# Keeping the transposed input of a two-block transformer kernel in DRAM instead of transposing it twice

## The chip, the cores and the metric

The kernel runs on one core of one Trainium2 chip. A core has five engines that run side by side, each working through its own list of instructions in order: TensorE (PE) for matrix products and transposes, VectorE (DVE), ScalarE (ACT), GpSimd (POOL), and SyncE (SP), which here only starts transfers. They meet through semaphores. The metric is device time of one execution in microseconds (us).

## The reference

Two transformer blocks follow each other on 512 tokens of width 1024, in float32. The part that matters here is the start and end of the first block's token mixer, and the memory projection of the second block, which the kernel does first of all:

```
h    = rmsnorm(x, norm_mix)                 # x: 512 x 1024
x    = x + hybrid_token_mixer(h, w_in, ...) # an mLSTM half and an RWKV half, then @ w_out
h    = rmsnorm(x, norm_x)                   # cross attention, feed-forward, ...
kv_m = rmsnorm(mem_2, g_mem_2) @ w_mem_kv_2 # 256 x 1024, from the second block
```

`rmsnorm(x, g)` is `x * rsqrt(mean(x*x) + 1e-6) * g`, row by row.

## The kernel before

Activations stand transposed in the kernel: model width on the 128 partitions, in 8 tiles (`KD`) of 128, and the 512 tokens along the free dimension. A float32 product is made of three passes: both operands are split into a rounded high part and a low part (`whi`, `wlo` for weights, `hh`, `hl` for activations), and high x high, high x low and low x high are added up in PSUM. A weight unit of 128x512 is loaded by SP into `wraw` (5 buffers), rounded by ACT into `whi`, and the rest made by DVE into `wlo` (3 buffers each).

A tile framework orders the instructions of each engine from the program order and priorities, and gives each its waits. Where `self.pinned` names an engine (`"pa"` in the opening: PE and ACT), that engine keeps the program's order. Tiles of a pool that was closed give their memory to later pools; an instruction that writes such memory waits for the last users of what lay there.

**The opening** (`start`, line 366). `x` and `mem_2` are loaded with tokens on partitions (`tok`). DVE or ACT sums squares, DVE computes `rs = rsqrt(mean + eps)` for six blocks of 128 tokens and multiplies each block of `x` by its `rs` in place (`scale`). The memory projection runs in two panels of 512 columns (`ch`), each in 8 steps over `k` of six matmuls. The steps of the second panel alternate with `turn` (line 461), which transposes tile `k` of the scaled `x` by four PE transposes into one PSUM bank (`p` and `q`, two of each) and evicts it twice: ACT writes `hh` (scaled by the norm's gain), DVE writes `hl` = the product less `hh`. Two further blocks of tokens, `mem`, are turned into `memT` in the same pool `st` and stored to `mem_kept`, and `kv_kept` holds the second block's memory keys and values. Both are DRAM tiles.

**The RWKV preparation** (`rwkv_prep`, line 570). Dense blocks of 24 matmuls follow each other on PE, one for every 128 columns of `w_in`. `shift` evicts a block twice on ACT (`sh`, whose first column POOL sets to 0, and `own`) and mixes them on DVE. The first shifted block becomes `lx`, the right side of the low-rank matmuls (`rank`), whose weights `lw`, `lwl` POOL prepares at the start, with `rst32`, a row pattern for a scan.

**The mixer's end** (`mixer_early`, line 1250, and `mixer_out`, line 1278). `x` is loaded a second time, tokens on partitions. The output projection goes over 8 tiles `m` of the result; behind the matmuls of each, four transposes of `x` go to a PSUM bank, ACT evicts them (`xs`, tile name `k`), and DVE adds them to the product in `xT`. ACT and DVE then make `hh` and `hl` of the cross attention from it.

Of the kernel before, what the change touches and what calls it, by code (L numbers as in the profile page):

```python
# [8 lines left out]
F32 = mybir.dt.float32  # L9
# [3 lines left out]
OP = mybir.AluOpType  # L13
# [3 lines left out]
S = 512  # L17
D = 1024
NB = S // 128
KD = D // 128  # L20
# [12 lines left out]
OE = 4  # L33
MY = 2
# [42 lines left out]
def weave(*gens):  # L77
    for _ in woven(*gens):
        pass
# [20 lines left out]
class Build:  # L100
# [265 lines left out]
    def start(self, st, yT, kept, hh, hl):  # L366
# [60 lines left out]
        ws = weights()  # L427
        wus = [next(ws), next(ws)]
        for ch, dst in ((0, km), (1, vm)):
            pss = [self.pm() for _ in range(2)]  # L430
            for k in range(KD):
                wu = wus.pop(0)
                wus.extend(part(ws, 1))
                self.dense_tok(pss, wu, (mh, mlo), (k,), k == 0, k == KD - 1, 512)
                if ch == 0:
                    if k < 3:
                        for b in range(2):
                            square((xs + m2)[(2 * k + 4 + b) % 6], (2 * k + 4 + b) % 6, b)
                    elif k == 3:
                        norms(0, 6)  # L440
                    else:
                        scale(xs[k - 4], k - 4)
                else:
                    self.turn(xs, k, k + 1, hh, hl, gc[:, 8:16])
            for s2 in range(2):
                self.act(dst[:, s2], pss[s2], AF.Copy, scale=rs[:, 4 + s2:5 + s2])
        self.pinned = ""
        self.head_norm(st, km, 4, 128, gkm, 2)
# [11 lines left out]

    def turn(self, xs, k0, k1, hh, hl, g):

        n = 128 * len(xs)
        per = 512 // n
        for k in range(k0, k1, per):
# [8 lines left out]
            if hl is not None:  # L474
                for m, pv, gm in cols:
                    self.stt(hl[:, m], pv, gm, hh[:, m].bitcast(F32), OP.mult, OP.subtract)


    def mixer(self, yT, hpool, kept):
# [13 lines left out]
        with tc.tile_pool(name="rk", bufs=1, reuse_waits=RW) as rk:  # L493
# [30 lines left out]
            with tc.tile_pool(name="ml", bufs=1, reuse_waits=RW) as ml:  # L524
# [6 lines left out]
                with tc.tile_pool(name="mid", bufs=1, reuse_waits=RW) as mid:  # L531
# [7 lines left out]
                    with tc.tile_pool(name="chain", bufs=1, reuse_waits=RW) as ch:  # L539
                        self.pinned = PIN[1]  # L540

                        self.turns = ["p", "s", "p", "y"]
                        weave(steps(CS, self.rwkv_chain(ch, TT, yT)), steps(XS + MY - LS - PS + 4 * OE, lstm, self.mixer_early(yT, rk)))
                self.pinned = ""
                self.turns, self.mms = ["p"], ["mm", "mm", "q", "q"]
                self.mixer_out(yT, rk, ml)

# [701 lines left out]

    def mixer_early(self, xT, rk):  # L1250

        nc, i = self.nc, self.i
        while not self.rw.get("read"):
            yield None
        x = self.tile(rk, [128, NB, D], "BK", 1)
        y = [self.tile(rk, [128, 2, 4, S], "KR", 1, F32R), None]
# [11 lines left out]
        parts(0)  # L1268
        for b in range(NB):
            nc.sync.dma_start(x[:, b], i["x"][0, 128 * b:128 * b + 128, :])  # L1270
        self.mms = ["mm", "mm", "q", "q"]
# [5 lines left out]

    def mixer_out(self, xT, rk, ml):
        x, y, half, early = self.outs
        y[1] = self.tile(rk, [128, 2, 4, S], "Gm", 1, F32R)  # L1280
        self.parts(1)
        for m in range(KD):
# [6 lines left out]
            for _ in half(ps, m, 1):  # L1289
                pass  # L1290
            p = self.pt()
            for b in range(NB):
                self.tr(p[:, 128 * b:128 * b + 128], x[:, b, 128 * m:128 * m + 128])
            xs = self.tile(ml, [128, 512], "k2", 2)
            self.act(xs, p)
            self.add(xT[:, m], xs, ps)

# [878 lines left out]
def kernel_body(ctx, tc, ins, out):  # L2176
# [4 lines left out]
    kd = ctx.enter_context(tc.tile_pool(name="kd", bufs=1, space=bass.MemoryType.DRAM))  # L2181
    kept = {n: kd.tile([128, 2048], F32, name=n + "_kept") for n in ("kv2", "mem", "k", "v")}
    ctx.enter_context(b.psum(mm=2, p=2, q=2, s=1, y=1))
    with tc.tile_pool(name="hp", bufs=1, reuse_waits=RW) as hp:
# [32 lines left out]
```

## Time and profile before

| | us |
|---|---|
| median of 3 runs | 1542.51 |
| lowest and highest | 1539.69, 1544.95 |
| the profiled execution, its own time | 1537.13 |
| its span, first to last instruction | 1535.4 |
| PE busy in the span | 1506.9 |
| DVE busy | 1082.0 |
| ACT busy | 748.7 |
| POOL busy | 98.9 |

The durations below come from the one profiled execution, whose time is 5.4 us under the median. A row of the timeline gives the start and the length of an instruction in us, its engine, its line in the kernel, output and inputs, and in brackets how long the engine had idled before it and what ended that. On PE the lengths overlap, since matmuls are pipelined: the distance from start to start counts there.

### The profile page before, as it was taken

How to read it: one execution, taken by the hardware profiler on the slowest of the kernel's cores; microseconds unless marked ns; L12 is line 12 of the kernel's file. 1: busy time of each engine (PE TensorE's matmuls, PEld its weight loads, DVE VectorE, ACT ScalarE, POOL GpSimd, SP SyncE). 2: the span in 40 equal slices, each digit the busy share in tenths (PEclk: the TensorE clock that was granted, in tenths of full speed). 3: DMA queues.
4: the chain of work that ended last, by engine and by line, in shares of the span. 5: the costliest groups of instructions: out<-in, count | busy, mean ns of one | idle time of the engine just before them, and what ended most of it. 6: DMA issues, size and time to landing. Idle time of an engine off the chain costs nothing.

```text
span 1535.4 us, 23728 instructions
## 1 busy us (share of the span) xinstructions
PE 1506.9 (98%) x8487; PEld 1237.2 (81%) x8487; DVE 1082.0 (70%) x2536; ACT 748.7 (49%) x1469; POOL 98.9 (6%) x241
## 2 busy tenths in 40 slices
PE   7999999999999999999999999999999999999999
PEld 5777788798888888888888888898877877878877
DVE  7776698998856556524544578879999785766563
ACT  6645556566554444434432444456554454644431
POOL 7000402122000000000000001000000000000000
PEclk9999999999999999999999999999999999999999
DMA  7533222145533133333333334242322322324222
GB/s 254 145 73 81 52 63 56 45 122 158 153 111 100 51 96 97 96 96 97 97 100 98 93 107 103 62 122 71 91 71 68 83 69 67 80 75 124 69 83 96
DMA packets 209591, 144.85 MB, mean 94 GB/s; under 512 B 13492, under 2 KB 190787, under 8 KB 208960
## 3 DMA queue, kind: packets, MB, share of 16 engines
q1 hardware_dynamic: 208000, 141.66, 32.6%
q0 software_dynamic: 1280, 1.52, 0.5%
q8 instruction: 67, 1.10, 0.3%
q14 instruction: 52, 0.43, 0.1%
q10 hardware_dynamic: 192, 0.14, 0.0%
HBM read 134.90 MB, written 8.39 MB: 93 GB/s over the span
## 4 chain that ended last, share of the span: by engine, by line
PE 85%; DVE 9%; ACT 2%; issue 1%; DMA 1%; DVEq 0%; SPq 0%; ACTq 0%
PE mm L180 39%; PE q L180 28%; PE p L188 4%; PE p L191 3%; PE y L188 3%; PE s L180 2%; DVE wlo L158 2%; PE s L188 2%; PE q L188 2%; PE s L191 1%; PE q L191 1%; DVE lqk L158 1%; DVE madd L1832 1%; ACT whi L155 1%; DVE m L1831 1%
## 5 line engine op out<-in xcount | busy, mean ns | idle before, releaser
L155 ACT ACTIVATE whi<-wraw 128x512 fp32r<-128x512 f32 (+2 forms) x472 | 292.5, 622 | 534.5 <-PE mm L180 216.2
L158 DVE TENSOR_TENSOR wlo<-wraw,whi 128x512 fp32r<-128x512 f32 (+2 forms) x472 | 320.3, 680 | 186.1 <-ACT whi L155 181.4
L180 PE MATMUL mm<-hh,whi 128*128 128x512 f32 (+1 forms) x760 | 281.2, 386 | 1.8 <-DVE hh L158 1.1
L180 PE MATMUL mm<-hh,wlo 128*128 128x512 f32 (+1 forms) x696 | 265.3, 381 | 0.0
L180 PE MATMUL mm<-hl,whi 128*128 128x512 f32 x632 | 247.2, 391 | 0.0
L180 PEld LDWEIGHTS mm<-hh,whi 128*128 128x128 f32 x760 | 138.9, 189 | 29.2 <-issue 3.0
L180 PEld LDWEIGHTS mm<-hh,wlo 128*128 128x128 f32 x696 | 131.0, 188 | 25.4
L180 PEld LDWEIGHTS mm<-hl,whi 128*128 128x128 f32 x632 | 119.2, 189 | 22.4 <-issue 0.5
L180 PE MATMUL q<-hh,whi 128*128 128x512 f32 x272 | 106.2, 391 | 0.0
L180 PE MATMUL q<-hh,wlo 128*128 128x512 f32 x272 | 106.0, 390 | 0.0
L180 PE MATMUL q<-hl,whi 128*128 128x512 f32 x272 | 106.0, 390 | 0.0
L180 PE MATMUL q<-whi,hh 128*128 128x512 f32 (+2 forms) x176 | 66.8, 388 | 0.0
L180 PE MATMUL mm<-whi,hh 128*128 128x512 f32 (+2 forms) x168 | 65.5, 396 | 0.0
L180 PE MATMUL q<-wlo,hh 128*128 128x512 f32 (+2 forms) x160 | 60.9, 381 | 0.0
L180 PEld LDWEIGHTS q<-hh,wlo 128*128 128x128 f32 x272 | 51.1, 188 | 10.6
L180 PEld LDWEIGHTS q<-hl,whi 128*128 128x128 f32 x272 | 51.1, 188 | 10.5
L180 PEld LDWEIGHTS q<-hh,whi 128*128 128x128 f32 x272 | 51.1, 188 | 10.4
L180 PE MATMUL mm<-wlo,hh 128*128 128x512 f32 (+2 forms) x152 | 57.9, 381 | 0.0
L180 PE MATMUL q<-whi,hl 128*128 128x512 f32 (+2 forms) x144 | 54.7, 380 | 0.0
L180 PE MATMUL mm<-whi,hl 128*128 128x512 f32 (+2 forms) x136 | 51.6, 380 | 0.0
L155 ACT ACTIVATE at_sm<-at_sm,at_mx 128x128 f32<-128x128 f32 (+3 forms) x64 | 35.7, 559 | 21.3 <-DVE at_mx L1598 20.9
L176 DVE SCALAR_TENSOR_TENSOR fy<-fc,vcols,fy 128x512 f32<-128x512 f32 x44 | 33.0, 751 | 9.2 <-ACT fy L155 8.5
(761 smaller groups left out, 3123.3 us busy)
## 6 DMA issues: line engine op xcount, KB each, us to landing
wraw<-in_w_in_dram SPq DMA_DIRECT2D x172, 256.0 KB, 2.9
wraw<-in_f_up_dram SPq DMA_DIRECT2D x88, 256.0 KB, 2.9
wraw<-in_f_down_dram SPq DMA_DIRECT2D x40, 256.0 KB, 2.8
wraw<-in_x_wkv_dram SPq DMA_DIRECT2D x32, 256.0 KB, 3.1
wraw<-in_w_out_dram SPq DMA_DIRECT2D x32, 256.0 KB, 2.7
wraw<-in_w_branch_dram SPq DMA_DIRECT2D x24, 256.0 KB, 2.7
wraw<-in_w_mem_kv_dram SPq DMA_DIRECT2D x16, 256.0 KB, 4.3
wraw<-in_x_wq_dram SPq DMA_DIRECT2D x16, 256.0 KB, 2.8
```

Source lines behind the costliest of these rows:

```text
L155: self.pin("a", self.nc.scalar.activation(out, in_, func, **kw))
L158: self.pin("v", self.nc.vector.tensor_tensor(out, a, b, op=op))
L176: self.pin("v", self.nc.vector.scalar_tensor_tensor(out, a, s, b, op0=op0, op1=op1))
L180: ins = self.nc.tensor.matmul(out, lhsT=a, rhs=b, start=start, stop=stop)
L188: self.pin("p", self.nc.tensor.matmul(out, lhsT=a, rhs=b, start=start, stop=stop))
L191: self.pin("p", self.nc.tensor.transpose(out, in_, self.ident if ident is None else ident))
L1831: nc.vector.max(m8, acc)
L1832: nc.vector.match_replace(acc, m8, acc, -3e38)
```

## The change

In the opening, `turn` gets a function `keep` that is called for each tile behind its two evictions: ACT evicts the bank a third time, unscaled, into `xk` (four buffers); POOL multiplies it by `full`; and POOL starts its store into a new DRAM tile `x_kept`. Since the transposed tile carries `rs`, `full` has to undo that: `root` is (mean + eps) times `rs`, which is 1/`rs`, and `row` makes of it, by four transposes and an eviction, a tile with the 512 values along the free dimension on all partitions. `mixer_early` loads `x_kept` in four transfers in place of `x`, and `mixer_out` adds it as it is.

```diff
+        root = st.tile([128, NB], F32, name="root")
+        full = st.tile([128, S], F32, name="full")
+        def keep(k, p):
+            t = self.tile(st, [128, S], "xk", 4)
+            self.act(t, p)
+            nc.gpsimd.tensor_tensor(t, t, full, op=OP.mult)
+            nc.gpsimd.dma_start(kept["x"][:, S * k:S * k + S], t)
...
                     elif k == 3:
                         norms(0, 6)
+                        self.mul(root, ss[:, 0:NB], rs[:, 0:NB])
...
-                    self.turn(xs, k, k + 1, hh, hl, gc[:, 8:16])
+                    self.turn(xs, k, k + 1, hh, hl, gc[:, 8:16], keep)
             for s2 in range(2):
                 self.act(dst[:, s2], pss[s2], AF.Copy, scale=rs[:, 4 + s2:5 + s2])
+            if ch == 0:
+                self.row(full, root)
...
+            if keep is not None:
+                for m, pv, gm in cols:
+                    keep(m, pv)
...
-        x = self.tile(rk, [128, NB, D], "BK", 1)
+        x = self.tile(rk, [128, KD, S], "BK", 1)
...
-        for b in range(NB):
-            nc.sync.dma_start(x[:, b], i["x"][0, 128 * b:128 * b + 128, :])
+        for k in range(0, KD, 2):
+            nc.sync.dma_start(x[:, k:k + 2].rearrange("p k t -> p (k t)"), kept["x"][:, S * k:S * k + 2 * S])
...
-            p = self.pt()
-            for b in range(NB):
-                self.tr(p[:, 128 * b:128 * b + 128], x[:, b, 128 * m:128 * m + 128])
-            xs = self.tile(ml, [128, 512], "k2", 2)
-            self.act(xs, p)
-            self.add(xT[:, m], xs, ps)
+            self.add(xT[:, m], x[:, m], ps)
...
+    kept["x"] = kd.tile([128, KD * S], F32, name="x_kept")
```

Three places in the engines' order show what moves. ACT in the second panel, before (`whi` is a weight's high part, `hh` the scaled input's; `p` and `q` are PSUM banks):

```order
L155 ACTIVATE hh_83<-q_360,gcols 128x512
L155 ACTIVATE whi_369<-wraw_367 128x512
L155 ACTIVATE hh_83<-p_379,gcols 128x512
L155 ACTIVATE whi_388<-wraw_386 128x512
L155 ACTIVATE hh_83<-q_398,gcols 128x512
L155 ACTIVATE whi_407<-wraw_405 128x512
```

and in the changed program:

```order
L155 ACTIVATE hh_84<-p_374,gcols 128x512
L155 ACTIVATE xk_381<-p_374 128x512
L155 ACTIVATE whi_387<-wraw_385 128x512
L155 ACTIVATE hh_84<-q_397,gcols 128x512
L155 ACTIVATE xk_404<-q_397 128x512
L155 ACTIVATE whi_410<-wraw_408 128x512
L155 ACTIVATE hh_84<-p_420,gcols 128x512
```

Between `hh` of a tile and the next weight stands the third eviction of the same bank; its waits name DVE's `hl` of that tile.

POOL at the end of the opening, before (`TT` holds the low-rank weights as loaded):

```order
L520 DMA xt<-in_r_g_up_dram 32x512
L581 MEMSET rst_641 128x512
L591 CAST lw_645<-TT 64x512
L582 MEMSET rst_641 128x16
L592 CAST lw_645<-TT 64x512
L593 TENSOR_TENSOR lwl<-TT,lw_645 64x512
```

and in the changed program, where eight such pairs (the last two shown) stand between the loads and the preparation:

```order
L436 TENSOR_TENSOR xk_490<-xk_490,full 128x512
L437 DMA x_kept<-xk_490 128x512
L436 TENSOR_TENSOR xk_507<-xk_507,full 128x512
L437 DMA x_kept<-xk_507 128x512
L597 MEMSET rst_683 128x512
L607 CAST lw_687<-TT 64x512
L598 MEMSET rst_683 128x16
L608 CAST lw_687<-TT 64x512
L609 TENSOR_TENSOR lwl<-TT,lw_687 64x512
```

The preparation of the low-rank weights went behind the stores. PE at the start of `mixer_out`, before (`Gm` holds the second half of the mixer's output, `BK` the input):

```order
L180 MATMUL mm_4924<-KR_4908,wlo_5018 128x512
L180 MATMUL mm_4921<-Gm_5037,whi_5048 128x512
L191 MATMUL p_5064<-ident,BK_4907 128x128 x4
L180 MATMUL mm_4921<-Gm_5037,whi_5048 128x512
L180 MATMUL mm_4921<-Gm_5037,wlo_5047 128x512
```

and in the changed program:

```order
L180 MATMUL mm_4966<-KR_4950,wlo_5060 128x512
L180 MATMUL mm_4963<-Gm_5079,whi_5090 128x512 x2
L180 MATMUL mm_4963<-Gm_5079,wlo_5089 128x512
L180 MATMUL mm_4963<-Gm_5079,whi_5090 128x512 x2
L180 MATMUL mm_4963<-Gm_5079,wlo_5089 128x512
```

All eight groups of four transposes are gone; the matmuls keep their order.

## Rows read from the trace of the kernel before

**Rows 1.** Page, part 1: busy time, share of the span, instructions.

```profile
PE 1506.9 (98%) x8487; PEld 1237.2 (81%) x8487; DVE 1082.0 (70%) x2536; ACT 748.7 (49%) x1469; POOL 98.9 (6%) x241
```

**Rows 2.** Stretches: length, busy us (instructions) by engine, granted clock, DMA share, GB/s.

```profile
34.00:44.00 10.00, 10.00 (x58) 8.30 (x56) 9.79 (x27) 6.69 (x12) 1.22 (x6) 1.00 0.59 137
410.00:447.50 37.50, 37.50 (x179) 30.29 (x177) 20.26 (x30) 18.61 (x31) 0.00 (x0) 1.00 0.30 88
```

**Rows 3.** The same view: the slice with the lowest clock in the opening.

```profile
30.00:32.00 2.00, 2.00 (x6) 1.61 (x6) 1.89 (x4) 1.21 (x2) 1.88 (x3) 0.50 0.34 120
```

**Rows 4.** Timeline of PE, second panel: turns 0, 1 and 7.

```profile
29.78 0.47 PE L191 MATMUL p<-ident,tok 128*128 128x128 f32 x1 [1.29 <-DVE tok L171]
...
32.60 0.60 PE L191 MATMUL q<-ident,tok 128*128 128x128 f32 x4
...
43.60 0.60 PE L191 MATMUL q<-ident,tok 128*128 128x128 f32 x4
```

**Rows 5.** Timeline of PE in the output projection, around one group of transposes.

```profile
429.01 0.60 PE L191 MATMUL p<-ident,BK 128*128 128x128 f32 x4
...
430.14 0.63 PE L180 MATMUL q<-KR,whi 128*128 128x512 f32 x2
...
430.85 0.63 PE L180 MATMUL q<-KR,whi 128*128 128x512 f32 x2
```

**Rows 6.** Timeline of SP: the last of the four loads of `x`.

```profile
382.96 1.30 SPq L1270 DMA_DIRECT2D BK<-in_x_dram  x1
```

**Rows 7.** Tile `k` in 410 to 450 us: ns min/median/max, first and last start.

```profile
L155 ACT ACTIVATE k<-p x8: 574/598/601, 412.2 to 447.8; 128x512 f32<-128x512 f32 x8
```

**Rows 8.** Timeline of ACT in the second panel.

```profile
36.91 0.69 ACT L155 ACTIVATE hh<-q,gcols 128x512 fp32r<-128x512 f32 x1 [0.62 <-PE q L191]
37.49 0.62 ACT L155 ACTIVATE whi<-wraw 128x512 fp32r<-128x512 f32 x1
```

**Rows 9.** Timeline of DVE in the opening.

```profile
25.68 2.43 DVE L171 TENSOR_SCALAR tok<-tok,nt_rs 128x1024 f32<-128x1024 f32 x3
...
31.02 0.75 DVE L176 SCALAR_TENSOR_TENSOR hl<-p,gcols,hh 128x512 fp32r<-128x512 f32 x1
...
38.44 0.68 DVE L158 TENSOR_TENSOR wlo<-wraw,whi 128x512 fp32r<-128x512 f32 x1
...
49.88 1.42 DVE L171 TENSOR_SCALAR tok<-tok,nt_rs 128x1024 f32<-128x1024 f32 x2
...
56.41 0.75 DVE L176 SCALAR_TENSOR_TENSOR rt<-sh,vcols,own 128x512 f32<-128x512 f32 x1
```

**Rows 10.** Timeline of POOL: a multiplication of a 128x512 tile in a later stage.

```profile
245.06 1.06 POOL L744 TENSOR_TENSOR DR<-ident,PC 128x512 f32<-128x512 f32 x1
```

**Rows 11.** Timeline of DVE at the same time.

```profile
245.12 1.03 DVE L214 TENSOR_SCALAR rs_i<-mvar 128x4 int32<-128x4 int32 x1
246.06 0.16 DVE L171 TENSOR_SCALAR rs_h<-mvar 128x4 f32<-128x4 f32 x1
```

**Rows 12.** Timeline of POOL: the preparation of the low-rank weights.

```profile
24.53 0.55 POOL L581 MEMSET rst<- 128x512 f32 x1
26.90 0.66 POOL L591 CAST lw<-TT 64x512 fp32r<-64x512 f32 x1 [1.82 <-DMA TT<-in_r_w_up_dram]
...
32.27 1.60 POOL L593 TENSOR_TENSOR lwl<-TT,lw 64x512 fp32r<-64x512 f32 x1
33.93 0.13 POOL L563 MEMSET sh<- 128x1 f32 x2
```

**Rows 13.** Timeline of PE: start of the second dense block, first low-rank matmul.

```profile
53.16 0.48 PE L180 MATMUL mm<-hh,whi 128*128 128x512 f32 x1
...
59.35 0.47 PE L188 MATMUL q<-lx,lw 128*128 128x512 f32 x1
```

**Rows 14.** Tile `memT`: its store, from issue to landing.

```profile
DMA to landing us min/median/max: 3.9/3.9/3.9
```

**Rows 15.** DMA issues: engine, count, KB each, median us from issue to landing.

```profile
rgu<-in_r_g_up_dram POOLq DMA_DIRECT2D x1, 256.0 KB, 5.6
```

More of the change, by code (lines that the diff above doesn't have):

```diff
@@ L459, in start, with turn @@
         nc.sync.dma_start(kept["mem"], mt.rearrange("p k t -> p (k t)"))
-    def turn(self, xs, k0, k1, hh, hl, g):
+    def turn(self, xs, k0, k1, hh, hl, g, keep=None):
         n = 128 * len(xs)
@@ L542, in mixer @@
                         self.turns = ["p", "s", "p", "y"]
-                        weave(steps(CS, self.rwkv_chain(ch, TT, yT)), steps(XS + MY - LS - PS + 4 * OE, lstm, self.mixer_early(yT, rk)))
+                        weave(steps(CS, self.rwkv_chain(ch, TT, yT)), steps(XS + MY - LS - PS + 4 * OE, lstm, self.mixer_early(yT, rk, kept)))
                 self.pinned = ""
                 self.turns, self.mms = ["p"], ["mm", "mm", "q", "q"]
-                self.mixer_out(yT, rk, ml)
+                self.mixer_out(yT, rk)
     def block(self, h, c0):
@@ L1247, in mem_kv, with mixer_early @@
                 nc.sync.dma_start(kept["v"].rearrange("p (s d) -> p s d", s=2)[:, s2, cc], t)
-    def mixer_early(self, xT, rk):
+    def mixer_early(self, xT, rk, kept):
         nc, i = self.nc, self.i
@@ L1276, in mixer_early, with mixer_out @@
         self.parts = parts
-    def mixer_out(self, xT, rk, ml):
+    def mixer_out(self, xT, rk):
         x, y, half, early = self.outs
```

## The prediction, made before the changed kernel ran

> **What bounds the kernel now.** The page first: TensorE is busy for 98% of the span [rows 1], so a matmul or transpose that is taken out is worth its place on PE, and a wait put in front of PE costs its full length. Then the two stretches that the change touches, by the view of busy time per stretch [rows 2]: the output projection of the mixer, 410 to 447.5 us, has PE at 37.50 of 37.50 us with ACT and DVE near half; the opening's second panel, 34 to 44 us, has PE at 10.00 of 10.00 but DVE at 9.79. The first stretch is PE's alone. In the second DVE has no room: what is pushed onto it, or holds it up, is pushed onto PE. [...]
>
> **What is taken away (mixer_out).** Eight groups of four transposes of `x`, with eight evictions on ACT that PE did not wait for. With a group in front, three matmuls take from 429.01 to 430.14, 1.13 us; the next three take from 430.14 to 430.85, 0.71 us [rows 5]. A group is worth 0.42 us, eight are worth **-3.4 us**. The stretch has no PE wait, so nothing hides this gain, and nothing is late behind it: the sum `xT = x + ps` now needs only the load, whose last part was issued at 382.96 [rows 6], over 25 us ahead of the stretch; the four loads keep their size of 512 KB and their place in SP's queue. ACT's eight evictions there cost nothing, as ACT idles half of it.
>
> **What is put in (opening).** One row `full` (four transposes, one eviction), eight evictions `xk`, eight POOL multiplications, eight POOL-issued stores. The four transposes stand ahead of the second panel, where PE waited for `tok` anyway; I cost them at nothing (0.4 us if that wait were gone). The small multiplication `root` on DVE is 0.2 us. Three things remain.
>
> (a) *A loop between ACT and DVE.* In the built program each `xk` waits for the `hl` of the same step, since both read one PSUM bank, and the next `whi` stands behind `xk` in ACT's order. So a step becomes a chain: `hh` 0.69, `hl` 0.75, `xk` at the price of the eviction `k<-p`, 0.60, `whi` 0.62 [rows 7 to 9]: 2.66 us, where PE now goes from turn to turn in (43.60 - 32.60)/6 = 1.83 us [rows 4]. Behind `whi` stand `wlo`, with PE behind that. From the first `xk` to the `wlo` of the last dense step this chain is passed five times; the first two steps have their weights already.
>
> To the 2.66 comes what POOL does to DVE. An `rs_i` of 4 columns took 1.03 us while POOL multiplied a 128x512 tile in 1.06 us; the `rs_h` behind it, without POOL, took 0.16 [rows 10, 11]. `hl`, which reads PSUM, took 0.75 us with POOL's casts beside it [rows 9]. [...] The rows bound the loss at 0 to 0.87 us for each multiplication (1.03 less 0.16); it is 0 where DVE's instruction starts first and POOL waits. DVE has work at nearly all times here, so I take 0.54, nearer to the upper row. A step is then 3.2 us, and five cost 5 x (3.2 - 1.83) = **+6.8 us**; the ends are 5 x (2.66 - 1.83) = +4.1 and 5 x (2.66 + 0.87 - 1.83) = +8.5.
>
> (b) *What DVE gains before it.* POOL's casts now run beside the four `tok` scalings: three take 2.43 us, and the last ends only before PE's turn at 29.78 [rows 4, 9]. In the changed order POOL waits for `xk` at that time, and the scalings stand together: two undisturbed ones take 1.42 us [rows 9], four some 2.75 us from 25.8, so the turn comes at 28.6 instead of 29.78, **-1.2 us**. PE idles less ahead of it; the step at the lower clock took 32.60 - 29.78 = 2.82 us, 1.0 us over the 1.83 [rows 4]. I take half of that back, **-0.5 us** (ends 0 and -1.0).
>
> (c) *POOL's preparation for the low-rank matmuls.* Now `rst32`, four casts and two `lwl` are done from 24.53 to 33.93 us [rows 12], 22 us before DVE's first shift at 56.41 [rows 9]. In the changed program they stand behind the eight multiplications and stores, and `rst32` lies on memory of the opening's `memT`, so it waits for the store of `memT` to land. Behind them on POOL's queue stands the memset of `sh`, which DVE's first shift waits for, and behind that the weight splits. Count from T, the start of the second dense block (53.16 now [rows 13]). The last `memT` eviction ends about T + 0.4 (worked out down ACT's new order); a weight split on ACT and one on DVE (0.62 and 0.68 [rows 8, 9]) stand ahead of an SP load, so the store is issued at T + 2.1 and lands 3.9 us later [rows 14], at T + 6.0. POOL's chain takes 9.4 us less the 1.8 it waited for a load [rows 12], 7.6, so `sh` is set at T + 13.6; from shift to the first low-rank matmul it takes 59.35 - 56.41 = 2.94 [rows 9, 13]: T + 16.5. PE gets there after 61 matmuls of 0.23 us (0.71 for three [rows 5]), T + 14.3. That is a stall of 2.2 us; were the two `lwl`, 1.60 us each, as quick as the multiplication of 1.06 [rows 10, 12], it would be 1.1. DVE is quieter in that time than it is now, so I take 1.6, and 0.2 for a slow spell behind it: **+1.8 us**, ends 1.1 and, with a whole slow spell of 1.0, 3.2. The later heads follow with the same spacing, and cost nothing more.
>
> The multiplications and stores themselves block nobody else: with four buffers a fifth `xk` is due some 10 us after the first store was issued, and a 256 KB transfer from POOL's queue landed in 5.6 us [rows 15].
>
> **The sum** against the profiled execution (1537.13 us by its own clock, span 1535.4): -3.4 + 6.8 - 1.2 - 0.5 + 1.8 = **+3.5 us**, 1540.6. That execution lies 5.4 us under the median of the runs, 1542.51; the same step from the median gives **1546.0 us**. All of the opening's delay reaches the end, since PE is bound behind it, with no long wait that could take it in.
>
> **The rivals.** *Slower, by POOL against DVE.* If nearly every multiplication shuts DVE out, (a) is +8.5, (c) 3.2 and PE's gaps keep the clock low, so that (b) gives back 0.3 only: -3.4 + 8.5 + 3.2 - 0.3 = +8.0, 1550.5 us. It decides from about 3.4 us a step in the second panel. For it speaks the row of `rs_i` [rows 11]; against it, that DVE's `hl` is free of it and that POOL loses some of the races. [...]
> *The opening hides it.* Weights are split two units ahead, and ACT has a third of its time free between 34 and 44 us [rows 2]. If the steps take no more than 2.2 us, (a) is +1.9 and, with (b) at -2.2 and (c) at 1.1, the whole is -2.6, 1539.9; below -4.6, faster by over 0.3%, it comes only if the panel ends earlier than now. For it speaks that `hl` is not wanted before the next stage; against it, DVE's 9.79 of 10.
> *The change does not do what it says*: the loads come too late and DVE waits for `x`. The issue at 382.96 [rows 6] leaves no room for that; 2%, within the other cases.
>
> **How the numbers follow.** 0.3% is 4.6 us, about what a measurement of this kernel can tell from no change; so faster means under 1537.9 and slower over 1547.1. The forecast, 0 to +6 us, has 55%, of which 15 lie above +4.6. The slower rival has 27%, all above it. The hidden case has 18%, 7 of them under -4.6. So faster 7%, the same 40 + 11 = 51%, slower 15 + 27 = 42%. The range reaches from -2.5 us, into the hidden case, to +9, just past the slower rival: 1540.0 to 1551.5.
>
> **What would show it.** In the trace of the changed kernel: no transposes of `x` between 410 and 450, and that stretch 3.4 us shorter; turns of the second panel 2.7 to 3.5 us apart instead of 1.83; DVE instructions of one microsecond beside each `xk` multiplication; POOL idle from its last store to the landing of `mem_kept`, then `rst32`, and PE waiting 1 to 2.2 us at its first low-rank matmul. Turns still 1.83 us apart would fell (a); a low-rank matmul without a wait would fell (c); an output projection that shrinks by less than 3 us would fell the gain.

## The result, and the profile of the changed kernel

The changed kernel takes 1551.3 us in the median of five runs (1547.7 to 1552.3), the kernel before, on the same chip, 1539.7 (1539.1 to 1545.0). The ratio is 1.0065, with a 95% interval from 1.0049 to 1.0080: slower by 10 us, 7.5 to 12.3. The profiled execution of the changed kernel has a span of 1549.1 us, 13.7 over the one of before.

The page, part 1 (busy time) and part 4 (shares of the chain that ended last, by engine), of the changed kernel:

```profile
PE 1510.2 (97%) x8459; PEld 1237.4 (80%) x8459; DVE 1085.2 (70%) x2537; ACT 748.2 (48%) x1470; POOL 113.1 (7%) x257
...
PE 84%; DVE 9%; ACT 2%; issue 2%; DMA 1%; POOL 0%; DVEq 0%; SPq 0%; ACTq 0%; POOLq 0%
```

TensorE has 28 matmuls fewer than in [rows 1] and still 3.3 us more of busy time; its mean granted clock is 0.994, before 0.996. Three stretches tell where the loss lies (the columns of [rows 2]): the second panel from turn 2 to turn 7, the wait ahead of the first low-rank matmul, and the stretch behind it.

```profile
33.50:52.00 18.50, 11.38 (x53) 7.91 (x52) 17.95 (x42) 8.32 (x16) 9.19 (x10) 1.00 0.46 128
74.00:80.00 6.00, 1.21 (x6) 0.72 (x4) 2.33 (x4) 2.27 (x4) 2.94 (x12) 1.00 0.09 16
80.00:87.00 7.00, 7.00 (x15) 4.38 (x15) 3.40 (x5) 3.08 (x6) 0.10 (x1) 0.51 0.25 62
```

In the panel PE is busy for 11.4 of 18.5 us, and DVE for 17.95. From 74 to 80 us PE stands nearly still, and the seven microseconds behind that ran at a granted clock of 0.51: 0.50 in each microsecond from 80 to 86 us, 0.60 in the next, and 1.00 from 87 us on. A stretch at about 0.50, as here and in [rows 3], is called one at the lower clock below.

The gain lies in the output projection, from its first matmul with `Gm` to the first matmul of the next stage. Timelines of PE, of the kernel before and of the changed one:

```profile
410.19 0.50 PE L180 MATMUL mm<-Gm,whi 128*128 128x512 f32 x1
...
411.73 0.60 PE L191 MATMUL p<-ident,BK 128*128 128x128 f32 x4
412.13 0.50 PE L180 MATMUL mm<-Gm,whi 128*128 128x512 f32 x1
...
447.48 0.47 PE L180 MATMUL mm<-hh,whi 128*128 128x512 f32 x1
```

```profile
427.10 0.49 PE L180 MATMUL mm<-Gm,whi 128*128 128x512 f32 x1
...
429.03 0.50 PE L180 MATMUL mm<-Gm,whi 128*128 128x512 f32 x1 [0.23 <-DVE Gm L158]
...
461.79 0.39 PE L180 MATMUL mm<-hh,whi 128*128 128x512 f32 x1
```

It took 37.3 us and takes 34.7, so 2.6 us less, not 3.4. Up to its third `Gm` matmul both kernels need 1.9 us: before, two groups of transposes stood there; now PE waits for DVE's `Gm` instead. Those two of the eight groups had cost nothing. Behind them the delay falls by 0.43 us at each of the other six.

The timeline of PE shows the places of the loss (turns 1, 2 and 7, one of the five waits between them, the start of the second dense block, and the first low-rank matmul); the rows that answer are [rows 4, 13]:

```profile
31.70 0.60 PE L191 MATMUL p<-ident,tok 128*128 128x128 f32 x4
33.52 0.60 PE L191 MATMUL q<-ident,tok 128*128 128x128 f32 x4
...
38.81 0.50 PE L180 MATMUL mm<-wlo,m2h 128*128 128x512 f32 x1 [1.40 <-DVE wlo L158]
...
52.03 0.60 PE L191 MATMUL p<-ident,tok 128*128 128x128 f32 x4
...
61.05 0.39 PE L180 MATMUL mm<-hh,whi 128*128 128x512 f32 x1
...
79.82 0.64 PE L188 MATMUL p<-lx,lw 128*128 128x512 f32 x1 [4.79 <-DVE lx L158]
```

From these, and from the same instructions found in both traces, the delay of the changed kernel against the kernel before can be followed through the program:

| at | before, us | changed, us | delay | since the line above |
|---|---|---|---|---|
| first matmul of the first panel | 11.63 | 12.12 | +0.5 | +0.5, the start of the run |
| its last matmul | 24.38 | 26.06 | +1.7 | +1.2, matmuls 0.43 us apart instead of 0.23 for 3 us longer |
| turn 0, last transpose | 29.78 | 30.14 | +0.4 | -1.3 |
| turn 2 | 34.44 | 33.52 | -0.9 | -1.3 |
| turn 7 | 43.60 | 52.03 | +8.4 | **+9.3** |
| second dense block | 53.16 | 61.05 | +7.9 | -0.5 |
| behind the low-rank matmuls | 133.7 | 149.3 | +15.5 | **+7.6** |
| start of the output projection | 410.19 | 427.10 | +16.9 | +1.4, granted clock 0.50 to 0.66 from 322 to 326 us |
| behind it | 447.48 | 461.79 | +14.3 | **-2.6** |
| behind PE's next wait | 478.19 | 491.74 | +13.5 | -0.8 |

Without the first two lines and the stretch at 322 us they add up to -1.3 - 1.3 + 9.3 - 0.5 + 7.6 - 2.6 - 0.8 = +10.4 us, which is what the runs say. The -0.8 is a wait of PE for DVE's `P`, 0.33 us instead of 1.03; in the mixer alone, below, the same wait is 1.36 us, so it is not shown to belong to the change. The other 3.3 us of this one execution (its start, its first panel, the lower clock at 322 us) are of the kind in which executions of one program differ: in the traces of the experiments below the delay at the end of the first panel is anything from -1.2 to +2.0 us, with the same instructions.

**The panel.** The chain of work that ended last, cut to one step and a half of it (start, length, what), does not pass through PE or ACT at all:

```profile
34.36 0.69 DVE wlo L158
35.05 0.66 DVE hl L176
...
36.62 1.14 DVE rs_t L158
...
38.68 0.75 DVE hl L176
39.42 0.67 DVE km L158 x2
...
40.54 1.76 DVE km L158
```

From 32.83 to 50.77 us this chain holds DVE's instructions, short pieces called "issue" and three of 0.02 us of DVE's queue, nothing else. ACT waits for DVE, and POOL's multiplications stand exactly where DVE's long instructions stand (timelines of ACT and of POOL):

```profile
35.74 0.60 ACT L155 ACTIVATE xk<-p 128x512 f32<-128x512 f32 x1 [2.01 <-DVE hl L176]
```

```profile
36.43 1.30 POOL L436 TENSOR_TENSOR xk<-xk,full 128x512 f32<-128x512 f32 x1 [1.50 <-ACT xk L155]
...
40.14 1.61 POOL L436 TENSOR_TENSOR xk<-xk,full 128x512 f32<-128x512 f32 x1 [1.52 <-ACT xk L155]
...
70.89 0.53 POOL L597 MEMSET rst<- 128x512 f32 x1 [10.61 <-DMA mem_kept<-memT]
...
75.44 1.26 POOL L609 TENSOR_TENSOR lwl<-TT,lw 64x512 fp32r<-64x512 f32 x1
76.76 0.13 POOL L579 MEMSET sh<- 128x1 f32 x2
```

`rs_t`, eight columns wide, takes 1.13 us beside the multiplication of 36.43 and 0.17 us elsewhere; a `km` takes 1.76 beside that of 40.14 and 0.68 elsewhere. Each of the five multiplications from 32.72 to 47.83 lengthened one DVE instruction by about a microsecond (0.96 to 1.08). `hl`, which reads PSUM, is not lengthened: the one at 56.29, beside POOL's multiplication of 55.88 to 57.19, takes 0.75, as in [rows 9].

**The first low-rank matmul.** The last three rows of POOL's timeline are the end of the chain that PE waited for: 10.6 us of waiting for the store of `memT`, then 6 us of work, then `sh`, on which DVE's first shift waited. SP's timeline, and the landing of that store (view of the tile `memT`):

```profile
60.40 0.50 SPq L463 DMA_DIRECT2D kv_kept<-xT  x1
...
63.03 1.14 SPq L472 DMA_DIRECT2D mem_kept<-memT  x1
```

```profile
DMA to landing us min/median/max: 7.7/7.7/7.7
```

It was 3.9 us in [rows 14]. Two stretches of the view by stretches stand beside it: of the changed kernel while the store was under way, and of the kernel before while its own was.

```profile
64.00:71.00 7.00, 7.00 (x32) 5.82 (x31) 2.16 (x4) 2.75 (x5) 0.11 (x1) 1.00 0.95 343
```

```profile
54.00:60.00 6.00, 5.89 (x26) 4.36 (x24) 3.75 (x14) 5.50 (x13) 0.22 (x4) 1.00 0.76 253
```

In the changed kernel the DMA engines are busy for 0.95 of the stretch, at 343 GB/s (before 0.76, 253 GB/s). The panel's delay had pushed the store of `kv` (1 MB, like that of `memT`) from 6.0 us ahead of it to 2.6 us ahead of it, with the last two stores of `x` and the weight loads beside both. The traces of the experiments below go the same way. Where the two stores are issued 5.2 us apart, that of `memT` lands after 5.2 us (`xk` a step later); 3.9 us apart after 5.8 (two placements mended, preparation late); 3.5 us apart after 6.7 (no multiplication); 2.8 us apart after 8.0 and 8.8 (opening alone; preparation behind the stores, no landing).

### The profile page after: what moved, and what is told of

Same layout as the page of the kernel before. It is cut to its first block, busy times and chain, and to the rows that moved or that the text cites. A ratio compares the mean times of both kernels' runs of the same rounds, so it can differ in the third digit from the quotient of the medians.

```text
span 1549.1 us, 23708 instructions
## 1 busy us (share of the span) xinstructions
PE 1510.2 (97%) x8459; PEld 1237.4 (80%) x8459; DVE 1085.2 (70%) x2537; ACT 748.2 (48%) x1470; POOL 113.1 (7%) x257
## 3 DMA queue, kind: packets, MB, share of 16 engines
q8 instruction: 66, 1.08, 0.3%
## 4 chain that ended last, share of the span: by engine, by line
PE 84%; DVE 9%; ACT 2%; issue 2%; DMA 1%; POOL 0%; DVEq 0%; SPq 0%; ACTq 0%; POOLq 0%
PE mm L180 39%; PE q L180 28%; PE p L188 4%; PE p L191 3%; PE y L188 3%; PE s L180 2%; DVE wlo L158 2%; PE q L188 2%; PE s L188 2%; PE s L191 1%; ACT whi L155 1%; DVE lqk L158 1%; DVE rs_t L158 1%; DVE madd L1843 1%; PE q L191 1%
## 5 line engine op out<-in xcount | busy, mean ns | idle before, releaser
L180 PEld LDWEIGHTS q<-hh,wlo 128*128 128x128 f32 x272 | 51.1, 188 | 10.6
L180 PEld LDWEIGHTS q<-hh,whi 128*128 128x128 f32 x272 | 51.1, 188 | 10.4
```

The costliest lines, as they stand in the source:

```text
L180: ins = self.nc.tensor.matmul(out, lhsT=a, rhs=b, start=start, stop=stop)
```

## The experiments

The theory after reading the two traces (A in most of the texts below): everything is lost in the opening, by three things that work on each other: the loop of evictions and weight splits that [rows 7 to 9] were read for, POOL's multiplications shutting DVE out, and the low-rank preparation that stands behind both and behind a store. The main rival: the loss comes from loading the stored copy, or one of the three does it alone. Times are medians; ratios are to the kernel before, run beside it on the same chip.

| kernel | median, us | before | ratio (95% interval) |
|---|---|---|---|
| opening alone | 1553.6 | 1541.1 | 1.0064 (1.0040 to 1.0087) |
| mixer alone | 1537.5 | 1541.1 | 0.9973 (0.9957 to 0.9988) |
| no multiplication | 1544.5 | 1541.1 | 1.0021 (1.0004 to 1.0037) |
| free memory | 1545.3 | 1541.1 | 1.0026 (1.0012 to 1.0040) |
| `xk` a step later | 1547.4 | 1541.3 | 1.0035 (1.0020 to 1.0049) |
| preparation behind the stores, no landing | 1545.6 | 1541.3 | 1.0023 (1.0012 to 1.0034) |
| all causes taken away | 1544.1 | 1541.3 | 1.0018 (1.0006 to 1.0029) |
| the same, loop kept | 1542.7 | 1541.3 | 1.0011 (1.0001 to 1.0020) |
| the same, preparation first | 1542.5 | 1541.3 | 1.0008 (0.9997 to 1.0019) |
| all, two placements mended | 1538.6 | 1541.3 | 0.9980 (0.9966 to 0.9993) |
| **the same, preparation late** | **1534.5** | 1541.3 | **0.9954 (0.9941 to 0.9967)** |
| before, preparation late | 1539.6 | 1541.3 | 0.9983 (0.9970 to 0.9996) |

### Opening alone, mixer alone

The first is the changed kernel with `mixer_early` and `mixer_out` of the kernel before; the copy is stored and never read. The second is the kernel before with this edit, which leaves the transposition out, so that the sum takes other elements of `x`:

```diff
-            p = self.pt()
-            for b in range(NB):
-                self.tr(p[:, 128 * b:128 * b + 128], x[:, b, 128 * m:128 * m + 128])
-            xs = self.tile(ml, [128, 512], "k2", 2)
-            self.act(xs, p)
-            self.add(xT[:, m], xs, ps)
+            self.add(xT[:, m], x[:, m // 2, S * (m % 2):S * (m % 2) + S], ps)
```

> The changed opening alone: the transposed input is scaled back, multiplied and stored as in the changed kernel, but the mixer loads the input as rows and transposes it on TensorE as before. Theory A (all of the loss is made in the opening and in the low-rank preparation behind it: 9.3 us in the five steps of the second panel, 4.8 us of idle TensorE before the first low-rank matmul and 3.6 us of half clock behind it, less some 3 us that the next block gives back): slower than the changed kernel by the 3.4 us of the mixer, so 13 to 16 us over the kernel before. Theory B (part of the loss comes from loading the stored copy for the mixer, or from the mixer without its evictions): no more than 10 us over the kernel before.

> The kernel before, whose mixer adds the loaded rows as they are: no transposition of the input and no eviction in the mixer's output (the transposition is left out, so the residual sum takes the wrong elements), and nothing is stored in the opening. Theory A (eight groups of four transposes lie on TensorE's path, 0.42 us each): 3.4 us below the kernel before, 2.5 to 4.3, all of it in the mixer's stretch. Theory B (the transposes ran in time that TensorE would have waited anyway): within 1 us of the kernel before.

The opening alone is 9.9 us over the kernel before by the ratio (6.2 to 13.4), 12.5 by the medians. 13 to 16 were expected, and up to 10 would have spoken for theory B, so the times do not decide between the two. Its trace does: the span is 2.8 us above the changed kernel's, with the same five waits in the panel and 5.0 us of wait at the first low-rank matmul. The opening carries the whole loss. The mixer alone gains 4.2 us by the ratio (1.8 to 6.6). In its trace the output projection takes 34.7 us, as in the changed kernel:

```profile
413.51 0.49 PE L180 MATMUL mm<-Gm,whi 128*128 128x512 f32 x1
...
448.22 0.39 PE L180 MATMUL mm<-hh,whi 128*128 128x512 f32 x1
```

So the load of the stored copy costs nothing that shows: in the changed kernel the delay stays at +16.9 us from 330 us, over the loads, to the start of the output projection. And the 2.6 us are all that the trace gives for the transposes; what the medians have beyond that isn't placed.

The trace of the mixer alone shows one thing more. Its opening is, instruction by instruction, that of the kernel before, yet the scalings of the token rows went worse than in [rows 9] (timeline of DVE):

```profile
26.56 3.73 DVE L171 TENSOR_SCALAR tok<-tok,nt_rs 128x1024 f32<-128x1024 f32 x3
...
31.23 1.75 DVE L171 TENSOR_SCALAR tok<-tok,nt_rs 128x1024 f32<-128x1024 f32 x1
```

Three took 3.73 us instead of 2.43, the fourth 1.75, and PE's turn 0 came at 33.03 instead of 29.78. The kernel before loses a varying amount here, and its one trace was among the better ones.

### No multiplication; `xk` a step later

```diff
-            nc.gpsimd.tensor_tensor(t, t, full, op=OP.mult)
```

> The changed kernel without the multiplication on GpSimd: the scaled tile is stored as it is (the undoing of the normalisation is left out). Theory A (each multiplication holds a VectorE instruction of the same step for about 1 us, and that lies in the loop of hh, hl, xk and the next weight): the five steps of the second panel take 2.7 us each, not 3.7, so 5 us below the changed kernel; the wait before the first low-rank matmul stays, since the preparation still waits for the stored memory tile to land. Theory B (the loop of evictions alone sets the steps, GpSimd only fills a gap): within 1 us of the changed kernel.

In the other kernel `keep` is called behind the next weight split of the panel's loop:

```diff
                 wus.extend(part(ws, 1))
+                while held:
+                    keep(*held.pop())
...
-                    self.turn(xs, k, k + 1, hh, hl, gc[:, 8:16], keep)
+                    self.turn(xs, k, k + 1, hh, hl, gc[:, 8:16], lambda *a: held.append(a))
```

> The changed kernel in which the third eviction of a bank (xk) stands one step later, behind the next weight's high part, so that ScalarE no longer waits for VectorE's hl of the same step before it makes the next weight; the multiplications on GpSimd stay. Theory A (the loop over hh, hl, xk and the next weight sets the steps, and the lock only lengthens it): the five steps fall from 3.7 us to what VectorE needs with its held instruction, 0.75 + 0.68 + about 1.0 = 2.4 us, so 5 to 7 us below the changed kernel. Theory B (the held VectorE instruction alone sets the steps, wherever the eviction stands): 3.3 us and more for a step, less than 2 us gained.

Turns 2 and 7 on PE, without the multiplication:

```profile
33.05 0.60 PE L191 MATMUL q<-ident,tok 128*128 128x128 f32 x4
...
46.51 0.60 PE L191 MATMUL p<-ident,tok 128*128 128x128 f32 x4
```

and with the eviction a step later:

```profile
32.25 0.60 PE L191 MATMUL q<-ident,tok 128*128 128x128 f32 x4
...
43.86 0.60 PE L191 MATMUL p<-ident,tok 128*128 128x128 f32 x4
```

Five steps: 13.46 / 5 = 2.69 us with the loop and no multiplication, 11.61 / 5 = 2.32 with the multiplication and no loop, 18.51 / 5 = 3.70 with both, 1.83 with neither (before). Alone, the loop adds 0.86 us a step and the held DVE instruction 0.49; together they add 1.87: the 3.70 is the 2.69 plus 1.01 for the multiplication of the step. Rival B of both texts falls.

How the loop acts is less plain than its mean. Without the multiplication the five steps are 1.83, 2.73, 3.06, 2.54 and 3.30 us, and in the chain of work from 33 to 47 us `whi` of ACT stands once, ahead of the step of 2.54:

```profile
40.55 0.63 ACT whi L155
```

In the other lengthened steps the chain is DVE's own list. The framework ordered that list differently in these kernels: between turns 2 and 7 DVE has four `km` and the scaling of a row tile with the loop, and one `km` before and with the eviction a step later, where the rest stands behind turn 7. So the 0.86 and the 0.49 are prices of these programs, the order of DVE's instructions included, and not of the loop and the held instruction by themselves.

Without the multiplication the time falls by 6.8 us, the panel by 5.0; the wait before the first low-rank matmul stayed (3.85 us), as expected. With the eviction a step later the panel gains 6.9 us, but the time only 4.6, and the trace 3.4 from turn 2 to behind the low-rank matmuls: PE then waited 2.4 us for `km` and 1.3 us for the scaled rows of `mem` (brackets in its timeline). A gain in front of a second wait of the same engine is in part only moved.

### Free memory; preparation behind the stores, no landing

```diff
-            t = self.tile(st, [128, S], "xk", 4)
+            t = m2[k // 2 % 2][:, S * (k % 2):S * (k % 2) + S]
...
-        full = st.tile([128, S], F32, name="full")
...
             if ch == 0:
+                full = self.tile(st, [128, D], "nt_junk", 2)[:, 0:S]
                 self.row(full, root)
```

> The changed kernel with the four copies in the memory of rows that are dead by then and the row of roots in that of the squares, so that the low-rank preparation on GpSimd writes no memory that the stored memory tile still holds and stands ahead of the multiplications, as in the kernel before. Theory A (the first low-rank matmul waited for that preparation, and the half clock followed from this idle stretch): no idle TensorE there and no half clock, 7 to 8.5 us below the changed kernel; of that about 1.2 us are lost again, since the casts run beside the scaling of the token rows as before. Theory B (the first low-rank matmul would then wait for something else that the late opening delays, a weight or the evictions on ScalarE): less than 3 us gained.

The other one has this too, and each instruction of the preparation ordered behind the eighth store.

> The changed kernel, multiplications and evictions as they are, with the copies in the memory of dead rows (so that the low-rank preparation overlies nothing that is still to be stored) and the preparation held behind the eighth store, where the changed kernel has it. It differs from the version with free memory in the place of the preparation alone, and from the changed kernel in not having to wait until the stored memory tile has landed. Theory A (the landing made the preparation late: 10.6 us of waiting for 6 us of work): the preparation runs from 60 to 67 us, TensorE waits 0 to 3 us before the first low-rank matmul, and the time is 5 to 8 us below the changed kernel. Theory B (standing behind eight multiplications and stores is enough by itself): TensorE still waits 4 us and more there, less than 3 us below the changed kernel.

Both are 6 us below the changed kernel; 7 to 8.5 had been expected of the first. With free memory the preparation was done by 31.7 us, and PE came to the first low-rank matmul without a wait; the scalings of the rows paid for it (timelines of DVE and PE):

```profile
26.79 5.49 DVE L171 TENSOR_SCALAR tok<-tok,nt_rs 128x1024 f32<-128x1024 f32 x4
```

```profile
70.40 0.45 PE L188 MATMUL p<-lx,lw 128*128 128x512 f32 x1
```

Behind the stores, without the landing, POOL worked from 60.8 to 67.2 us, and PE waited 2.6 us instead of 4.8 (timelines of POOL and PE):

```profile
60.82 0.54 POOL L600 MEMSET rst<- 128x512 f32 x1
...
65.88 1.29 POOL L612 TENSOR_TENSOR lwl<-TT,lw 64x512 fp32r<-64x512 f32 x1
```

```profile
70.02 0.47 PE L188 MATMUL p<-lx,lw 128*128 128x512 f32 x1 [2.64 <-DVE lx L158]
```

So the landing was the larger part: without it, at the same place, the time is 6 us lower, and in the trace the delay grows by 3.3 us from the second dense block to behind the low-rank matmuls instead of 7.6. The place behind the stores is worth the rest there, and is paid back by scalings that nobody disturbs: the two kernels take the same time.

### All causes taken away, and two parts put back

The eviction a step later, free memory, the preparation behind the last store, and the multiplication moved into the mixer, where the row `full` is loaded from DRAM:

```diff
+            self.mul(x[:, m], x[:, m], full)
             self.add(xT[:, m], x[:, m], ps)
```

> All causes taken away at once, with the transposed input still stored and no transposition in the mixer: the eviction a step later, the multiplication by the row of roots moved to VectorE in the mixer's output (eight of some 0.7 us, the row stored and loaded as 256 KB), the copies in the memory of dead rows, and the low-rank preparation on GpSimd behind the last store. Theory A (loop, lock and the late preparation are all that the change cost): steps of the second panel at ScalarE's 0.62 + 0.69 + 0.60 = 1.9 us, no idle TensorE before the first low-rank matmul, 3.4 us off the mixer: 2 to 5 us below the kernel before. Theory B (VectorE becomes the limit of the mixer's output, which had 20 of 37 us busy there): the mixer's stretch is as long as before, and the whole within 1 us of the kernel before or above.

> As the version with all causes taken away, but with the third eviction in its place directly behind hl of the same step. Theory A (the loop has a price of its own, without any lock: 0.69 + 0.75 + 0.60 + 0.62 = 2.7 us a step): 4 us above the version with the eviction a step later. Theory B (without the multiplication the loop is hidden in the time that TensorE waits anyway): within 1 us of it.

> As the version with all causes taken away, but the low-rank preparation on GpSimd stands where the scheduler puts it when its memory is free, ahead of the stores and beside the scaling of the token rows, as in the kernel before. Theory A (the casts on GpSimd hold the scalings on VectorE: four of them took 9.2 us in the kernel before and 2.74 us each in a row undisturbed): the first turn of the second panel 1 to 2.5 us later, so 1 to 2.5 us above the version with the preparation behind the stores. Theory B (the scalings are hidden by the first panel): no difference.

These were misses. The first was to be 2 to 5 us faster than the kernel before and is 2.8 us slower. Its panel did what it should: turns 2 and 7 at

```profile
33.85 0.60 PE L191 MATMUL q<-ident,tok 128*128 128x128 f32 x4
...
44.86 0.60 PE L191 MATMUL p<-ident,tok 128*128 128x128 f32 x4
...
62.39 0.47 PE L188 MATMUL p<-lx,lw 128*128 128x512 f32 x1 [2.59 <-DVE lx L158]
```

2.20 us a step (1.9 in the first four, 3.3 in the last), and at the second dense block it stood 1.0 us behind the kernel before. Then it lost 3.2 us at the low-rank matmuls (last row, with a granted clock of 0.65 from 62 to 66 us), since the preparation behind the eighth store ended at 59.3 us; 3.0 in a stretch at the lower clock at 182 us (0.66 in the mean of 180 to 190); and 3.9 ahead of the mixer, where the scheduler had put multiplications into the end of the chunk chain (timeline of DVE; `BK` is the loaded `x`, `k` the row):

```profile
399.17 0.69 DVE L158 TENSOR_TENSOR BK<-BK,k 128x512 f32<-128x512 f32 x1
...
400.45 0.68 DVE L158 TENSOR_TENSOR BK<-BK,k 128x512 f32<-128x512 f32 x1
```

With the loop kept, the steps were 2.71 us (turn 2 at 32.67, turn 7 at 46.20), so the loop has its price without any multiplication, as its theory A says, 2.5 us for the panel. The time does not show it: this kernel is 1.4 us below the one without the loop, inside both intervals; its profiled execution has a mean granted clock of 0.996 instead of 0.994, and 1.6 us of wait at the low-rank matmul instead of 2.6. With the preparation first the scalings were held as expected,

```profile
28.84 4.48 DVE L171 TENSOR_SCALAR tok<-tok,nt_rs 128x1024 f32<-128x1024 f32 x4
```

4.48 us instead of 2.74, and the kernel was not slower but 1.6 us faster: it saved the 2.6 us at the low-rank matmul. (The 9.2 us that its text gives for the scalings of the kernel before are wrong: three took 2.43 us [rows 9], the fourth 1.09.) The three times can't be told apart; what they share, a loss of 3.9 us ahead of the mixer, was the finding.

### Two placements mended

The multiplication of a row is ordered behind the sum of the row ahead of it, and the preparation behind the fifth store, or behind the seventh:

```diff
+            if k == 4:
+                self.stored = ins.ins.name
...
+            ins = self.nc.vector.tensor_tensor(x[:, m], x[:, m], full, op=OP.mult)
+            self.after(ins, self.last)
```

> The version with all causes taken away, with two placements mended: the low-rank preparation on GpSimd begins behind the fifth store instead of the eighth, and the multiplication of each row on VectorE stands directly ahead of its sum instead of ahead of the chain's last normalisation, where TensorE had waited 2.6 us for VectorE's gg. Theory A (these two placements ate the gain: 2.6 us of idle TensorE and a half-clock spell before and behind the first low-rank matmul, and 3.9 us ahead of the mixer): 5 to 8 us below that version, so 2 to 5 us below the kernel before. Theory B (casts in the second panel hold VectorE as the multiplications did, and the steps there lengthen to 2.5 us and more): 3 us lost again in the panel, about the kernel before.

> As the version with two placements mended, but with the low-rank preparation behind the seventh store. Theory A of that version: the panel's steps are free of it (1.9 us), and the first low-rank matmul waits about 1 us; within 2 us of it. Theory B: 2 to 3 us below it, since no cast runs beside the second panel.

Both are faster than the kernel before, the second by 7.1 us (5.1 to 9.1) and by 17 us than the changed kernel. In its trace the multiplications fit beside PE's work (view of the tile `k`: ns min, median, max, first and last start), the delay against the kernel before falls by 2.6 us over the output projection and by 1.1 at the wait behind it, and the wait at the first low-rank matmul is 0.4 us (timeline of PE):

```profile
L1319 DVE TENSOR_TENSOR BK<-BK,k x8: 684/687/687, 414.7 to 442.2; 128x512 f32<-128x512 f32 x8
```

```profile
59.62 0.47 PE L188 MATMUL p<-lx,lw 128*128 128x512 f32 x1 [0.43 <-DVE lx L158]
```

Why the fifth store is worse than the seventh by 4 us in the medians is seen in part. The panel's steps are the same, but with the fifth PE waits 2.7 us for the scaled rows of `mem` (at 49.6 us), with the seventh 0.4: the casts then stand beside DVE's norm of these rows, in which a `rs_t` takes 1.14 us. From turn 2 to behind the low-rank matmuls the first loses 1.4 us more. The two traces differ by 0.8 us in their own time; the rest of the 4 us stays open.

### Before, preparation late

```diff
+                    if k == KD - 1:
+                        self.stored = nc.gpsimd.memset(xs[0][:, 0:1], 0.0).ins.name
```

> The kernel before, nothing stored and the mixer with its transpositions, in which only the low-rank preparation on GpSimd is held behind the last turn of the second panel (by a memset of one column of a dead row tile), so that no cast runs beside the scaling of the token rows. It tells how much of the best version's 7 us belongs to that placement and not to the stored input. Theory A (the casts beside the scalings cost the kernel before 1.2 us in its profile and more in other runs, where TensorE waited up to 3.9 us for them): 1 to 4 us below the kernel before. Theory B (the placement is worth nothing without the rest): within 1 us of it.

2.6 us below the kernel before (0.6 to 4.6). The scalings were nearly undisturbed:

```profile
26.10 2.08 DVE L171 TENSOR_SCALAR tok<-tok,nt_rs 128x1024 f32<-128x1024 f32 x3
```

In its one trace the 1.2 us that this saved were gone again at the next wait, at 45 us, so how they reach the end in the median isn't shown. Of the best version's 7.1 us (5.1 to 9.1), then, about 2.6 (0.6 to 4.6) belong to a placement that the kernel before could have had without any stored input, and some 4.5 to the stored input, whose gain in the mixer is 2.6 by the trace and 4.2 (1.8 to 6.6) by the runs. Well placed, storing costs nothing that these runs can tell.

## Why the prediction was right and wrong

The time, 1551.3 us, lies at the upper edge of the range, 1540.0 to 1551.5, and that is luck in part: the range goes to +9 us from a median of 1542.5, but the kernel before, run beside the changed one, took 1539.7, and the step is +10. The likeliest case (+3.5 us, no change) did not come; the rival "slower, by POOL against DVE" did, and went past its own numbers.

- **What is taken away, -3.4 us: the price of a group right, their number not.** A group gave 0.43 us (0.42 was said), but six gave it, not eight: 2.6 us in the changed kernel and in the mixer alone. "The stretch has no PE wait, so nothing hides this gain" was the wrong step. Before, PE was busy there without a break because two groups of transposes filled the time in which it would have waited for DVE's `Gm`. That the trace has -3.4 us in all comes from the shorter wait behind the stretch, and is luck. The loads were in time.
- **(a), the loop, +6.8 us: the mechanism right, the size not.** It measured +9.3, above the upper end of 8.5. The chain without POOL was put at 2.66 us a step and measured 2.69 in the mean, but that agreement is chance in part: the steps went from 1.83 to 3.30, and most of them followed DVE's own list. Where the chain did pass through ACT its members are others than I said: DVE's order has the next `wlo` ahead of the next `hl`, so it runs `xk`, `whi`, `wlo`, `hl`, and `hh` (0.68) lies beside `wlo` (0.69). The term that failed is POOL's: I took 0.54 us of 0 to 0.87 for a multiplication, since POOL would lose some of the races. It lost none that mattered: 1.01 us a step. Behind turn 7 it lost one: DVE's `wlo` of 53.16, begun ahead of POOL's multiplication of 53.43, took its 0.68 us, and POOL's 1.56 instead of some 1.3. The 0.87 was too low as an end as well, because it was read from a multiplication of 1.06 us, and here they took 1.27 to 1.61 [rows 10, 11]. The row of `rs_i` had shown it, 4 columns in 1.03 us [rows 11]; in the panel instructions eight columns wide took 1.13 us, and a `km` 1.76, against 0.17 and 0.68 elsewhere. Weighing the 0.87 down by a guess on who starts first was the mistake; DVE, with 98% work [rows 2], had an instruction standing there each of the five times.
- **(b), undisturbed scalings, -1.2 and -0.5 us: right in kind, and a little more.** Four took 2.74 us in a row (2.75 was said), and gave 1.3 us at turn 0. The granted clock, before 0.50 in 30 to 32 us [rows 3], stayed at 1.00 from 28 to 54 us, which with the quicker turns gave another 1.3 up to turn 2. That PE waited for `root` now (1.1 us) where it had waited for `tok` made the four added transposes free, as costed. No run shows the low clock that the slower rival put behind PE's gaps in the panel: PE waited there five times, 0.75 to 1.95 us, and the granted clock was 1.00.
- **(c), the late preparation, +1.8 us: the mechanism right, the size wrong by a factor of four.** Counted from T, now 61.05 us: the store was issued at T + 2.0 (T + 2.1 said), PE reached the low-rank matmul at T + 14.0 (T + 14.3 said). But the store landed at T + 9.7 instead of T + 6.0, the term that failed: its 3.9 us came from a place where the DMA engines were busy for 0.76 of the time [rows 14], and the delay that (a) makes moves another store of 1 MB up against it. POOL's work was quicker than said (6 us, not 7.6), so the matmul came at T + 18.8 (T + 16.5 said) after 4.8 us of idle PE. Behind an idle stretch of that length came seven microseconds at a granted clock of 0.51, 2.8 us more for the same matmuls; I had allowed 0.2, at most 1.0. That the kernel without the landing, its preparation still behind the stores, is 6 us faster shows the landing as the main cause; that the crowded DMA engines (0.95 busy) made it late rests on the rows of the two stretches and on the landings in the other traces, and was not tried by itself.
- **The sum.** 10.4 measured against 3.5: 2.5 from (a), 5.8 from (c), less 1.4 from (b) and from the -0.5 behind the panel; the mixer's part came out as forecast only with the wait behind it. The two large misses are one: both took a price from one place of the trace before (a multiplication of 1.06 us [rows 10], a landing of 3.9 [rows 14]), and at the place of the change it was higher (1.27 to 1.61, and 7.7).

## What to carry to other kernels

Work that is moved off the bounding engine must be priced on the engine that takes it, at the load that this engine has there: here a POOL multiplication beside a DVE that is busy 97% of the time cost DVE a microsecond, even in an instruction eight columns wide. An eviction that waits for another engine's reading of the same bank belongs behind the next piece of work that somebody waits for, not ahead of it: here that took 6.9 us off the panel and 4.6 off the time. And look what the moved step's memory overlies and what stands behind it in its queue: here a preparation that stood behind eight stores and the landing of a ninth cost 7.6 us where the transposes were worth about 3, and the same change, with its multiplication in another stage and the preparation placed well, was 17 us faster. Last, an engine without a wait in a stretch is no proof that each instruction there costs its length: look at what the next one would wait for if it were gone.

## What was not expected of the hardware

Behind the same short waits of PE the granted clock fell in one trace and stayed in another. In the kernel before PE waited 0.38 and 0.51 us at 177 to 178 us, and the clock was 1.00 from there to 188 us; in the version with all causes taken away PE waited 0.38 and 0.50 us at the same instructions and then ran 180 to 190 us at a mean granted clock of 0.66, which cost 3.0 us. The changed kernel lost 1.4 us in the same manner at 322 us, at 0.50 to 0.66 for four microseconds, behind waits of 0.67 and 1.08 us that the kernel before had as well, at 1.00 from 300 to 320 us. Differences of 1.5 to 3 us between single traces of these kernels are thus no evidence on an edit; the medians of several runs are.
